# Row softmax on one core: loads 6 and 7 issued by ScalarE, between two loops of exponentials

## The chip, the core and the metric

The kernel runs on one core of a Trainium2 chip. Its engines run beside each other and meet through semaphores: VectorE (DVE in the profile), ScalarE (ACT), GpSimd (POOL), SyncE (SP), and TensorE (PE), which has no part in this kernel. Data moves between the device's memory (HBM) and the core's on-chip memory (SBUF, 128 partitions) by 16 DMA engines. A transfer is issued by an instruction of an engine and goes into a queue of that engine; here SP issues all of them.

The metric is the time on the device in microseconds (us), from runs on the chip. One further execution is profiled; its trace gives the single instructions, the DMA shares, and the span from its first to its last instruction.

## The reference

```python
def reference(x):                      # x: (16, 1024, 512) float32
    x_max = np.max(x, axis=-1, keepdims=True)
    exp_x = np.exp(x - x_max)
    return (exp_x / np.sum(exp_x, axis=-1, keepdims=True)).astype(np.float32)
```

A softmax over the last axis: 16,384 rows of 512 numbers. 33.55 MB are read and as many written.

## The kernel before

**Tiling.** The 16,384 rows are 128 "rows" of each of the 128 partitions. They are cut into 16 groups of 8 (`GROUP`, `GROUPS`), and for the transfers into 8 blocks of 16, so two groups to a block (`BLOCKS`). One transfer moves a block: 128 partitions, 32 KB in one piece for each, 4 MB. The on-chip buffer `held` has room for 12 groups (`RING`, 96 rows), that is 6 blocks. Block 6 goes into the place of block 0, block 7 into that of block 1, when these have been stored. In the text load 6 is the load of rows 96 to 112, load 7 that of rows 112 to 128; store 0 is the store of rows 0 to 16, and so on.

**A group's way.** VectorE takes the negated maximum of each row (`rowmax`, line 171; step M in `VECTOR`) and counts up `maxed`. ScalarE waits for that and does eight exponentials in place with the row's sum beside them (lines 210 to 223; one loop over 16 groups, with the row's place in `held` worked out from the loop's index), and counts up `expd`. VectorE takes the reciprocal of the sums (line 179), and the product of the rows with it (line 185) is made by GpSimd for groups 0 to 11 (steps P) and by VectorE for groups 12 to 15 (steps V). The product counts up `scaled[g]`. The order of VectorE's steps is written out by hand in `VECTOR`; its end is M12 M13 V12 M14 V13 M15 V14 V15.

**SP's queue.** SP issues the transfers in the order of `ORDER`: loads 0 to 5 ahead (`AHEAD`), then stores 0, 1, 2, loads 6 and 7, stores 3 to 7. Before a store it waits until both groups of the block are scaled. `AFTER` adds later groups to wait for: group 4 before store 0, group 8 before load 6, group 9 before load 7, group 11 before store 3, group 12 before store 5. Before load 6 and load 7 it also waits until store 0 and store 1 have landed (lines 152 to 155). At the end it waits for the stores that nothing waited for yet (lines 226 to 228). `take` (line 115) is a wait for a semaphore that takes the count off again; most waits carry that line in the trace.

**Whom the loads serve.** The first maximum of a block waits for its load (`take` in `rowmax`): M12 for load 6, M14 for load 7.

Of the kernel before, what the change touches and what calls it, by code (L numbers as in the profile page):

```python
# [8 lines left out]
EXP = mybir.ActivationFunctionType.Exp  # L9
# [4 lines left out]
GROUP = 8  # L14
GROUPS = 16
RING = 12 * GROUP

# [2 lines left out]
ORDER = [  # L22
    ("L", (0, 16)),
    ("L", (16, 32)),
    ("L", (32, 48)),
    ("L", (48, 64)),
    ("L", (64, 80)),
    ("L", (80, 96)),
    ("S", (0, 16)),
    ("S", (16, 32)),  # L30
# [9 lines left out]
AHEAD = 6  # L40

AFTER = {("S", 0): 4, ("L", 96): 8, ("L", 112): 9, ("S", 48): 11, ("S", 80): 12}

# [28 lines left out]
@with_exitstack  # L77
def kernel(
    ctx: ExitStack,
    tc: tile.TileContext,  # L80
    x: bass.AP,
    out: bass.AP,
):
    nc = tc.nc
    nc.at_finalize(loads_at_the_head)
    P = nc.NUM_PARTITIONS

    d = x.shape[-1]
    x_rows, out_rows = x.flatten_outer_dims(), out.flatten_outer_dims()
    assert x_rows.shape[0] == GROUPS * GROUP * P  # L90

    def in_dram(rows, a, b):

        first, last = next(k for k in BLOCKS if k[0] <= a and b <= k[1])
        block = rows[first * P : last * P].rearrange("(p r) d -> p r d", p=P)
        return block[:, a - first : b - first, :]

    held = nc.alloc_sbuf_tensor("held", [P, RING, d], F32).ap()
    shift = nc.alloc_sbuf_tensor("shift", [P, GROUPS * GROUP], F32).ap()
    sums = nc.alloc_sbuf_tensor("sums", [P, GROUPS * GROUP], F32).ap()  # L100
    recip = nc.alloc_sbuf_tensor("recip", [P, GROUPS * GROUP], F32).ap()

    loads = [k for what, k in ORDER if what == "L"]
    stores = [k for what, k in ORDER if what == "S"]
    loaded = {k: nc.alloc_semaphore(f"loaded{k[0]}") for k in loads}
    scaled = [nc.alloc_semaphore(f"scaled{g}") for g in range(GROUPS)]
    stored = {k: nc.alloc_semaphore(f"stored{k[0]}") for k in stores}
    maxed = nc.alloc_semaphore("maxed")
    expd = nc.alloc_semaphore("expd")
    to_pool = nc.alloc_semaphore("to_pool")  # L110
    to_vector = nc.alloc_semaphore("to_vector")

    def take(engine, semaphore, n):

        engine.wait_ge(semaphore, n).then_inc(semaphore, -n)  # L115

    def rows(a, b):
        assert a // RING == (b - 1) // RING
        return held[:, a % RING : (b - 1) % RING + 1, :]

    def meets(k, a, b):
        return k[0] < b and a < k[1]

    def group(g):
        return g * GROUP, (g + 1) * GROUP

    def stats(t, g):
        return t[:, g * GROUP : (g + 1) * GROUP]

    def load(k):  # L130
        copy = nc.sync.dma_start(out=rows(*k), in_=in_dram(x_rows, *k))
        copy.then_inc(loaded[k], 16)
        return copy

    with tc.manual_schedule():
        for _, k in ORDER[:AHEAD]:
            tc.no_tile_sem_insts.add(load(k).ins.name)  # L140
    tc.close()
    tc.compile()  # L142

    taken, done = set(), set()
    for what, k in ORDER[AHEAD:]:
        for g in range(GROUPS):
            due = AFTER.get((what, k[0])) == g or (what == "S" and meets(k, *group(g)))
            if due and g not in done:
                take(nc.sync, scaled[g], 1)
                done.add(g)  # L150
        if what == "L":
            for s in stores:
                if meets(s, k[0] - RING, k[1] - RING) and s not in taken:
                    take(nc.sync, stored[s], 16)
                    taken.add(s)
            load(k)
        else:
            nc.sync.dma_start(out=in_dram(out_rows, *k), in_=rows(*k)).then_inc(
                stored[k], 16
            )  # L160

    seen, given = set(), {}

    def rowmax(g):
        for k in loads:
            if meets(k, *group(g)) and k not in seen:
                take(nc.vector, loaded[k], 16)
                seen.add(k)  # L170
        nc.vector.reduce_max(  # L171
            out=stats(shift, g), in_=rows(*group(g)), axis=AX, negate=True
        ).then_inc(maxed, 1)

    def scale(g, engine, ready):

        if g == 0:
            take(nc.vector, expd, 1)
        ratio = nc.vector.reciprocal(out=stats(recip, g), in_=stats(sums, g))  # L179
        if g:  # L180
            ratio.wait_op(expd, g, "sem-ge")
        ratio.then_inc(ready, 1)
        if g == 0:
            take(engine, ready, 1)
        product = engine.tensor_mul(  # L185
            out=rows(*group(g)),
            in0=rows(*group(g)),
            in1=stats(recip, g).unsqueeze(2).to_broadcast([P, GROUP, d]),
        )
        if g:  # L190
            given[ready] = given.get(ready, 0) + 1
            product.wait_op(ready, given[ready], "sem-ge")
        product.then_inc(scaled[g], 1)

    for step in VECTOR.split():
        what, g = step[0], int(step[1:])
        if what == "M":
            rowmax(g)
        elif what == "V":
            scale(g, nc.vector, to_vector)  # L200
        else:
            scale(g, nc.gpsimd, to_pool)
    take(nc.vector, expd, GROUPS - 1)
    take(nc.vector, to_vector, given[to_vector])
    take(nc.gpsimd, to_pool, given[to_pool])


    nc.scalar.preload_act_table(EXP)  # L208

    with nc.scalar.Fori(0, GROUPS) as i:  # L210
        take(nc.scalar, maxed, 1)
        for r in range(GROUP):
            row = held[:, bass.ds(i % (RING // GROUP) * GROUP + r, 1), :]
            at = bass.ds(i * GROUP + r, 1)
            act = nc.scalar.activation(  # L215
                out=row,
                in_=row,
                func=EXP,
                bias=shift[:, at],
                scale=1.0,  # L220
                accum_out=sums[:, at],
            )
        act.then_inc(expd, 1)


    for k in stores:
        if k not in taken:
            take(nc.sync, stored[k], 16)
# [30 lines left out]
```

## Time and profile before

| | us |
|---|---|
| median of 3 runs | 159.43 (159.36 to 159.45) |
| the profiled execution | 159.46 |
| its span | 158.1 |
| GpSimd's 12 products | 83.7 |
| VectorE's 16 maxima | 70.3 |
| VectorE's 4 products | 17.7 |
| ScalarE's 128 exponentials | 90.3 |

67.11 MB pass the DMA engines, at a mean of 424 GB/s over the span. In the page, a line's start and length are in us from the first instruction; "L171" is line 171 of the kernel; a name with a q behind the engine is an instruction of its sequencer (issue of a DMA, wait, register). The row marked DMA cuts the span into 40 equal slices and gives, in tenths, how busy the 16 DMA engines were. "us to landing" runs from a transfer's issue until its last byte has arrived, so it contains the time for which the transfer stood behind others in the queue.

### The profile page before, as it was taken

How to read it: one execution, taken by the hardware profiler on the slowest of the kernel's cores; microseconds unless marked ns; L12 is line 12 of the kernel's file. 1: busy time of each engine (PE TensorE's matmuls, PEld its weight loads, DVE VectorE, ACT ScalarE, POOL GpSimd, SP SyncE). 2: the span in 40 equal slices, each digit the busy share in tenths (PEclk: the TensorE clock that was granted, in tenths of full speed). 3: DMA queues.
4: the chain of work that ended last, by engine and by line, in shares of the span. 5: the costliest groups of instructions: out<-in, count | busy, mean ns of one | idle time of the engine just before them, and what ended most of it. 6: DMA issues, size and time to landing. Idle time of an engine off the chain costs nothing. (4 is left out here: it accounts for less than half of the span.)

```text
span 158.1 us, 720 instructions
## 1 busy us (share of the span) xinstructions
DVE 90.0 (57%) x36; ACT 92.0 (58%) x257; POOL 83.9 (53%) x16
## 2 busy tenths in 40 slices
DVE  0008959778977977977700000695999996920000
ACT  0300699999999999999994000049946839000000
POOL 0000009999999999999999999991000000000000
DMA  7999999999999999999999999999999999999996
GB/s 265 439 472 414 406 464 456 398 414 481 431 398 423 472 431 398 423 489 414 398 439 489 381 414 398 439 472 414 398 448 472 406 398 439 481 406 414 464 448 265
DMA packets 2304, 67.11 MB, mean 424 GB/s; under 512 B 256, under 2 KB 256, under 8 KB 256
## 3 DMA queue, kind: packets, MB, share of 16 engines
q1 hardware_dynamic: 2304, 67.11, 99.0%
HBM read 33.55 MB, written 33.55 MB: 424 GB/s over the span
## 5 line engine op out<-in xcount | busy, mean ns | idle before, releaser
L215 ACT ACTIVATE held<-held,shift x128 | 90.3, 709 | 38.7 <-ACTq L115 38.7
L185 POOL TENSOR_TENSOR held<-held,recip 128x4096 f32<-128x4096 f32 x12 | 83.7, 7016 | 23.1 <-POOLq L115 23.1
L171 DVE TENSOR_REDUCE shift<-held 128x8 f32<-128x4096 f32 x16 | 70.3, 4401 | 27.3 <-DVEq L115 27.3
L215 ACT ACTIVATION_READ_ACCUMULATOR held<-held,shift x128 | 24.2, 189 | 0.0
L185 DVE TENSOR_TENSOR held<-held,recip 128x4096 f32<-128x4096 f32 x4 | 17.7, 4425 | 0.1
L179 DVE RECIPROCAL recip<-sums 128x8 f32<-128x8 f32 x16 | 3.2, 202 | 21.9 <-ACT held L215 20.0
L208 ACT ACT_TABLE_LOAD x1 | 1.3, 1283 | 3.9 <-PEq L142 3.9
L243 POOL MEMSET const-float32-0.0<- 128x1 f32 x1 | 0.1, 98 | 0.2 <-issue 0.2
L243 POOL MEMSET const-bfloat16-1.0<- 128x1 bf16 x1 | 0.1, 101 | 0.0
L243 POOL MEMSET const-uint8-127<- 128x1 uint8 x1 | 0.1, 101 | 0.0
L243 POOL MEMSET const-float32-1.0<- 128x1 f32 x1 | 0.1, 98 | 0.0
## 6 DMA issues: line engine op xcount, KB each, us to landing
held<-in_x_dram SPq DMA_DIRECT2D x8, 4096.0 KB, 25.8
out_dram<-held SPq DMA_DIRECT2D x8, 4096.0 KB, 21.2
```

Source lines behind the costliest of these rows:

```text
L171: nc.vector.reduce_max(out=stats(shift, g), in_=rows(*group(g)), axis=AX, negate=True).then_inc(maxed, 1)
L179: ratio = nc.vector.reciprocal(out=stats(recip, g), in_=stats(sums, g))
L185: product = engine.tensor_mul(out=rows(*group(g)), in0=rows(*group(g)), in1=stats(recip, g).unsqueeze(2).to_broadcast([P, GROUP, d]),)
L208: nc.scalar.preload_act_table(EXP)
L215: act = nc.scalar.activation(out=row, in_=row, func=EXP, bias=shift[:, at], scale=1.0, accum_out=sums[:, at],)
L243: nc = _bacc.Bacc("TRN2", target_bir_lowering=False, num_devices=1)
```

## The change

Loads 6 and 7 leave SP's queue. ScalarE issues them in its own queue, after the exponentials of group 11 and before those of group 12; before each of them it waits until the store whose place it takes has landed. The loop of ScalarE over 16 groups becomes two loops, of twelve groups and of four, with a plain index into `held`. SP issues the stores alone, from store 0 on in the same order; its waits for groups 8 and 9 now stand before store 4, as that store's own.

```diff
-AFTER = {("S", 0): 4, ("L", 96): 8, ("L", 112): 9, ("S", 48): 11, ("S", 80): 12}
+AFTER = {(0, 16): 4, (48, 64): 11, (80, 96): 12}
...
-    def load(k):
-        copy = nc.sync.dma_start(out=rows(*k), in_=in_dram(x_rows, *k))
+    def load(k, engine):
+        copy = engine.dma_start(out=rows(*k), in_=in_dram(x_rows, *k))
         copy.then_inc(loaded[k], 16)
         return copy
...
-            tc.no_tile_sem_insts.add(load(k).ins.name)
+            tc.no_tile_sem_insts.add(load(k, nc.sync).ins.name)
...
-    taken, done = set(), set()
+    done = set()
     for what, k in ORDER[AHEAD:]:
+        if what == "L":
+            continue
         for g in range(GROUPS):
-            due = AFTER.get((what, k[0])) == g or (what == "S" and meets(k, *group(g)))
-            if due and g not in done:
+            if (meets(k, *group(g)) or AFTER.get(k) == g) and g not in done:
                 take(nc.sync, scaled[g], 1)
                 done.add(g)
-        if what == "L":
-            for s in stores:
-                if meets(s, k[0] - RING, k[1] - RING) and s not in taken:
-                    take(nc.sync, stored[s], 16)
-                    taken.add(s)
-            load(k)
-        else:
-            nc.sync.dma_start(out=in_dram(out_rows, *k), in_=rows(*k)).then_inc(
-                stored[k], 16
-            )
+        nc.sync.dma_start(out=in_dram(out_rows, *k), in_=rows(*k)).then_inc(
+            stored[k], 16
+        )
...
-    with nc.scalar.Fori(0, GROUPS) as i:
-        take(nc.scalar, maxed, 1)
-        for r in range(GROUP):
-            row = held[:, bass.ds(i % (RING // GROUP) * GROUP + r, 1), :]
-            at = bass.ds(i * GROUP + r, 1)
...
+    def exps(groups, first):
+        with nc.scalar.Fori(0, groups) as i:
+            take(nc.scalar, maxed, 1)
+            for r in range(GROUP):
+                row = held[:, bass.ds(i * GROUP + r, 1), :]
+                at = bass.ds(i * GROUP + first + r, 1)
...
+    exps(RING // GROUP, 0)
+    taken = set()
+    for what, k in ORDER[AHEAD:]:
+        if what == "L":
+            for s in stores:
+                if meets(s, k[0] - RING, k[1] - RING) and s not in taken:
+                    take(nc.scalar, stored[s], 16)
+                    taken.add(s)
+            load(k, nc.scalar)
+    exps(GROUPS - RING // GROUP, RING)
```

The body of the loop, the activation with its sum, is otherwise the same.

More of the change, by code (lines that the diff above doesn't have):

```diff
@@ L208 @@
     nc.scalar.preload_act_table(EXP)
-    with nc.scalar.Fori(0, GROUPS) as i:
-        take(nc.scalar, maxed, 1)
-        for r in range(GROUP):
-            row = held[:, bass.ds(i % (RING // GROUP) * GROUP + r, 1), :]
-            at = bass.ds(i * GROUP + r, 1)
[L215 to L223, printed above, removed]
+    def exps(groups, first):
[4 more added lines that the diff above has]
+                at = bass.ds(i * GROUP + first + r, 1)
+                act = nc.scalar.activation(
+                    out=row,
+                    in_=row,
+                    func=EXP,
+                    bias=shift[:, at],
+                    scale=1.0,
+                    accum_out=sums[:, at],
+                )
+            act.then_inc(expd, 1)
+    exps(RING // GROUP, 0)
[8 more added lines that the diff above has]
+    exps(GROUPS - RING // GROUP, RING)
     for k in stores:
```

## The prediction

> **What bounds the kernel now.** I read the page's head first, then its row of DMA shares, then the queue's part.
>
> ```profile
> span 158.1 us, 720 instructions
> DVE 90.0 (57%) x36; ACT 92.0 (58%) x257; POOL 83.9 (53%) x16
> ...
> DMA  7999999999999999999999999999999999999996
> ...
> q1 hardware_dynamic: 2304, 67.11, 99.0%
> ```
>
> No engine is busy for 60% of the span, while the 16 DMA engines are full in every slice but the first and the last, and one queue accounts for all of it. The kernel is bound by its bytes. The profile's chain that ended last covers only a few us before 139.5 and then stops at the issue of the last store, because it doesn't follow a transfer that waits behind other transfers; so I rebuilt the order of the transfers from the timeline of SP's queue and from each issue's time to landing.
>
> ```profile
> 0.00 3.14 SPq L131 DMA_DIRECT2D held<-in_x_dram  x6
> 58.51 7.30 SPq L158 DMA_DIRECT2D out_dram<-held  x3
> 86.47 7.31 SPq L131 DMA_DIRECT2D held<-in_x_dram  x2
> 107.32 32.48 SPq L158 DMA_DIRECT2D out_dram<-held  x5
> ```
>
> Issue plus time to landing gives: load 0 at 12.2 us, load 5 at 60.8 (2.7 + 58.1), store 0 at 70.5 (58.5 + 12.0), store 1 at 80.1 (59.0 + 21.1), store 2 at 90.4 (65.5 + 24.9), load 6 at 100.0 (86.5 + 13.5), load 7 at 109.7 (93.4 + 16.3), store 3 at 119.4 (107.3 + 12.1), and store 7 at 158.1 (139.5 + 18.6), which is the end of the span. So 16 transfers of 4 MB follow each other at about 9.7 us: 12.2 + 15 x 9.73 = 158.1. Each is issued before its predecessor ends; the closest is store 3, issued at 107.3 while load 7 lands at 109.7, a margin of 2.4 us. A change can move the end only if it leaves the DMA engines without work, or changes what a packet costs them.
>
> Packets do not always cost the same. The windows view (us, engines' busy time, clock, share of the 16 engines, GB/s) around the turns from loads to stores and back:
>
> ```profile
> 0.00:1.00 1.00, 0.00 (x0) 0.00 (x0) 0.20 (x4) 1.00 0.00 0
> 0.00:5.00 5.00, 0.00 (x0) 1.06 (x1) 0.20 (x4) 1.00 0.84 315
> 9.70:19.40 9.70, 7.04 (x2) 2.26 (x7) 0.00 (x0) 1.00 1.00 432
> 58.00:63.00 5.00, 3.90 (x3) 5.00 (x16) 5.00 (x2) 1.00 0.98 419
> 87.00:92.00 5.00, 0.00 (x0) 0.00 (x0) 5.00 (x1) 1.00 0.92 354
> 107.00:112.00 5.00, 3.16 (x3) 5.00 (x17) 0.22 (x1) 1.00 0.97 419
> ```
>
> A row's share x length x 16 is engine time, its GB/s x length is bytes, and a big packet is 32,768 bytes (4096 KB over the 128 of a transfer; 2304 packets are 16 x 144, 128 of them data and 16 of a few bytes). In a steady stretch (9.7 to 19.4): 128 packets in 155.2 us of engine time, 1.21 us each. At 87 to 92, where store 2 gives way to load 6: 1.77 MB are 54 packets in 0.92 x 5 x 16 = 73.6 us, 1.36 us each. The excess, 54 x 0.15 = 8 us over 16 engines, is 0.5 us. At the start, with no store about: 48 packets in 67.2 us, excess 9 us, 0.55 us for each engine. Where a load gives way to a store (58 to 63, 107 to 112): 64 packets in 78.4 and 77.6 us, excess 1 and 0 us, at most 0.06 us. So a beginning stream of loads costs about 0.5 us, with or without stores before it, and a beginning stream of stores costs nothing that shows.
>
> **The change, part by part.** *The two issues move to ScalarE.* SP loses two DMA issues (0.34 us each) and the waits for stored 0 and 1, and takes scaled 8 and 9 later, before store 4. ScalarE gets the two issues and two waits: 2 x 0.34 to 0.49 us (the range of load issues on SP) + 2 x 0.02 (a wait of ScalarE's queue took 17 ns) = 0.7 to 1.0 us. What stands behind them in ScalarE's queue is the exponentials of group 12, for which it waits anyway:
>
> ```profile
> 84.77 0.18 ACT L215 ACTIVATION_READ_ACCUMULATOR held<-held,shift  x1
> ...
> 100.14 8.74 DVE L171 TENSOR_REDUCE shift<-held 128x8 f32<-128x4096 f32 x2 [14.94 <-DVEq L115]
> 104.90 0.72 ACT L215 ACTIVATE held<-held,shift  x1 [19.94 <-ACTq L115]
> ...
> 115.27 4.41 DVE L171 TENSOR_REDUCE shift<-held 128x8 f32<-128x4096 f32 x1
> ```
>
> The waits are open when it comes to them: store 0 landed at 70.5, store 1 at 80.1, the twelfth group ends at 85.0. So both loads are issued by about 86, under 19.94 us of idle time. Cost 0; without that cover, 1 us on the path to group 12.
>
> *The second loop and the plain index.* A few register instructions (29 ns a MOVE, 35 an ALU_OP, 40 to 45 a branch) come and go, under 0.2 us, in the same idle time. If the longer program has to be fetched at the loop's end, no row here prices it; 0 below, and above the 4.5 us from 85 to 90.4 would pass unseen, since store 2 still has work. I take 0. The second queue may cost something at the start or end of the program. What lies outside the span is 159.46 - 158.1 = 1.4 us in all; nearest are SP's waits at the barrier, 0.4 us, so 0 to 0.4; I take 0, as nothing in the loop's issue touches the barrier.
>
> *When SP's stores go.* Store 0 still waits for scaled 4, stores 1 and 2 for scaled 3 and 5, store 3 for scaled 11 (POOL, 12 x 7.0 us from 23.5, to 107.2). SP no longer waits between, but store 3 had its wait last at 107.3 already. Gain 0.
>
> *Two queues at once.* This is the only part that reaches the bound. The first bytes moved not before 1.0 us after the first issue (the window 0 to 1), so load 6 comes into play at 86.1, and store 2 has 90.4 - 86.1 = 4.3 us of work left. If both queues share evenly, store 2 lands near 94.7 instead of 90.4; nobody waits for it but the end. Load 6 has then done 4.3 of its 9.7 us, goes on alone, and lands at 100.0 as before. Load 7 goes alone until store 3 comes in at 107.3 + 1.0 = 108.3 with 1.4 us of it left: it lands at 111.1 instead of 109.7. Who waits for load 7 is the maximum of group 14, at 115.27, held there by VectorE's own product of group 12; 4.2 us of cover remain. Had it none, 1.4 us would pass down the chain to store 7, whose issue at 139.5 lies 8.9 us ahead of 148.4, where store 6 ends. Cost 0. The Trainium skill, in "DMA: Bandwidth & Descriptors" (Queues, rings and completion order), says that each engine goes round the queues that have work, one packet each; by that rule the sharing is even and the landings are these, and no run shown has two data queues at once. The Trainium skill, on that page (Issuing engines are not separate DMA queues), says that a second issuing engine saves only issue time; by that the sum is 0, as here.
>
> What a packet costs while both queues are at work is not in the trace. Below: the loads begin under a running store stream and the whole 0.5 us at 87 to 92 goes, -0.5. Above: each return from a store's packet to a load's costs as much as the one return at 87 to 92. Shared packets per engine are 4.3 / 1.21 + 1.4 / 1.21 = 4.7 returns; 4.7 x 0.5 = 2.35, less the 0.5 already paid, +1.85. I take 0: the start shows the 0.5 us without any store, so it belongs to a stream that begins, and one stream of loads still begins, once. The turns from load to store, where engines of both kinds run beside each other for some tenths of a us, show no excess.
>
> **Sum.** 0 (issues) + 0 (loop) + 0 (stores) + 0 (sharing) on the profiled 159.46 (span 158.1); the runs' median is 159.43, so it is typical. Forecast 159.4.
>
> **Rivals.** *The beginning of the loads is hidden.* For it: load 6 starts 4.3 us earlier, beside a store that keeps each engine busy. Against: at 87 to 92 the load had been issued before store 2 ended and still paid. 159.4 - 0.5 = 158.9.
>
> *Returning to loads costs (the other side).* Engines alternate packet by packet from 86.1 to 94.7 and from 108.3 to 111.1. For it: the only return in the trace cost 0.5 us. Against: the start's 0.55 without stores. The kernel is slower as soon as a return costs over 0.5 / 4.7 = 0.11 us; at 0.17 it is +0.3 (159.75), at 0.5 +1.85 (161.3). I put its middle at 160.3.
>
> *The stores' queue goes first.* Then load 7's last 1.4 us wait behind stores 3, 4 and 5 (3 x 9.7 from 108.3) until about 138.8. Groups 14's maximum (4.4), VectorE's product 13 (4.4 + 0.2), maximum 15 (4.4), the exponentials of 15 (5.7), product 15 (4.6) put store 7's issue at 162.5; 1.0 + 9.7 more is a span of 173, a time of 174.5. Nothing in the rows speaks for it. If the loads go first, load 6 and 7 come 5 us sooner, store 2 later, and the time stays.
>
> *The change doesn't do what it says* if ScalarE's issues came after 90.4; the waits above exclude it, and the time would be the same until 5 us later still.
>
> **Chances.** The forecast 0.42, beginning hidden 0.22, returns cost 0.33, stores first 0.03. Over 0.2% (0.32 us) is about what a measurement can tell from no change. So faster 0.22, same 0.42, slower 0.33 + 0.03 = 0.36. The range goes from 158.8 (the hidden case, 0.1 for scatter) to 160.9 (most of the returns' case); outside are the upper third of that case, the stores-first case and a little below, some 0.16. The forecast's own range is 159.1 to 159.7.
>
> **What would show it.** Two load issues on ScalarE's queue at 85 to 86; store 2's time to landing up from 24.9 to about 29, load 7 landing near 111, group 14's maximum still at 115.3; the DMA row without a dip. In the hidden case the window 87 to 92 goes from 0.92 and 354 GB/s to some 430. In the returns' case GB/s falls in 86 to 95 and again in 108 to 111, and everything behind it shifts by the same amount. It would be wrong if the shared stretch lost over 0.3 us, or if the time outside the span grew.

## The result, and the profile after

The changed kernel takes 160.24 us (median of 6 runs, 159.95 to 160.59), the kernel before, run beside it, 159.44: a ratio of 1.0048, 95% interval 1.0031 to 1.0065. It is slower by 0.8 us, where no change was forecast. The profiled execution took 159.96 us, with a span of 158.6 where before had 158.1. It is one of the two fastest of the six, so its trace shows 0.5 of the 0.8 us.

The page of the changed kernel, its head and its DMA queues:

```profile
span 158.6 us, 721 instructions
DVE 90.0 (57%) x36; ACT 92.0 (58%) x257; POOL 83.9 (53%) x16
...
DMA  7999999999999999999999999999999999999996
...
q1 hardware_dynamic: 2016, 58.72, 86.7%
q10 hardware_dynamic: 288, 8.39, 12.4%
q14 instruction: 1, 0.01, 0.0%
```

The engines' work is the same to 0.1 us and the DMA row still has no dip. What is new is the queue q10, ScalarE's, with the two loads, and one fetch of instructions (q14). The timeline of the issues, with the last instruction of group 11's exponentials:

```profile
81.01 0.38 ACTq L131 DMA_DIRECT2D held<-in_x_dram  x1
...
81.51 1.18 ACTq L131 DMA_DIRECT2D held<-in_x_dram  x1
...
84.81 0.19 ACT L212 ACTIVATION_READ_ACCUMULATOR held<-held,shift  x1
...
107.35 3.25 SPq L152 DMA_DIRECT2D out_dram<-held  x2
```

ScalarE's sequencer issued the loads at 81.0 and 81.5, while its exponentials ran until 85.0: it runs ahead of them, and store 1 had landed at 80.2. Issue plus time to landing: store 2 at 95.4 (65.5 + 29.9; before 90.4), load 6 at 100.4 (before 100.0), load 7 at 110.1 (109.7), store 3 at 119.9 (119.4), store 7 at 158.6 (158.1). So 0.4 us were there by load 6's end and 0.5 by store 3's. The windows view shows where:

```profile
58.00:63.00 5.00, 3.90 (x3) 5.00 (x16) 5.00 (x2) 1.00 0.97 419
82.00:87.00 5.00, 0.20 (x1) 3.00 (x10) 5.00 (x2) 1.00 0.93 328
87.00:92.00 5.00, 0.00 (x0) 0.00 (x0) 5.00 (x1) 1.00 1.02 439
92.00:97.00 5.00, 0.00 (x0) 0.00 (x0) 5.00 (x2) 1.00 1.02 439
...
107.00:112.00 5.00, 3.20 (x3) 5.00 (x15) 0.25 (x1) 1.00 0.99 408
```

Read as in the prediction (share x length x 16 over the packets that the GB/s make): 82 to 87 has 50 packets in 74.4 us, 1.49 us each instead of 1.21, which is 0.86 us lost for each engine; 107 to 112 has 62 packets in 79.2 us, 1.28 each, 0.25 us lost. Load 6's first packet starts at 85.6, and store 2's last at 92.7; of that stretch the view of the queues says:

```profile
q10 hardware_dynamic: 46, 1.51, 52.5%
q1 hardware_dynamic: 44, 1.44, 47.0%
```

So load 6 had 46 packets and store 2 had 44, and followed engine by engine they alternate one by one. From 87 to 97 a packet costs 1.22: alternating is free. The slow packets start at 84 to 86: they are store 2's last ones ahead of the alternating and load 6's first. Before, the one loss was 0.5 at 87 to 92. So load 6's beginning lost 0.86 instead of 0.5, and store 3's beginning 0.25 instead of 0.

### The profile page after: what moved, and what is told of

Its sections match the earlier page's. It is cut to its first block, busy times and chain, and to the rows that moved or that the text cites. A ratio compares the mean times of both kernels' runs of the same rounds, so it can differ in the third digit from the quotient of the medians.

```text
span 158.6 us, 721 instructions
## 1 busy us (share of the span) xinstructions
DVE 90.0 (57%) x36; ACT 92.0 (58%) x257; POOL 83.9 (53%) x16
## 3 DMA queue, kind: packets, MB, share of 16 engines
q1 hardware_dynamic: 2016, 58.72, 86.7%
```

## The experiments

Lost time below is the sum over a stretch's big packets of what each took above 1.213 us (a packet of a steady stretch), divided by 16 engines, from the packets in each trace. It comes from one execution of each kernel, the ratio from 4 to 12 runs. Six kernels have load 6 in SP's queue at 86.4 to 86.7 and stores 0 to 2 ahead of it at the old times (before, e1, e4, e6, e8, e11); they lost 0.33 to 0.55 at load 6, so two traces that differ by 0.2 there show no difference. "Before" in each comparison is the kernel before, run beside the other.

| kernel | ratio to before (95%) | lost at load 6's beginning | lost at store 3's | elsewhere |
|---|---|---|---|---|
| before | 1 | 0.48 | 0 | |
| the change | 1.0048 (1.0031 to 1.0065) | 0.87 | 0.23 | |
| e1 | 0.9999 (0.9989 to 1.0009) | 0.35 | 0 | |
| e2 | 1.0044 (1.0027 to 1.0060) | 0.42 | 0.53 | |
| e3 | 1.0072 (1.0049 to 1.0096) | 0.85 | 0.39 | |
| e4 | 0.9999 (0.9990 to 1.0008) | 0.53 | 0 | |
| e5 | 0.9996 (0.9987 to 1.0005) | 0.35 | 0 | |
| e6 | 1.0121 (1.0106 to 1.0137) | 0.33 | engines idle | |
| e7 | 1.0217 (1.0200 to 1.0235) | 0.46 | 0.60 | store 7 issued late |
| e8 | 1.0060 (1.0040 to 1.0080) | 0.33 | 0 | 0.26 at the small loads |
| e9 | 1.0046 (1.0033 to 1.0059) | 0 | 0.23 | 0.62 before store 0 |
| e10 | 1.0003 (0.9994 to 1.0011) | 0.44 | 0 | |
| e11 | 1.0001 (0.9992 to 1.0010) | 0.55 | 0 | |
| e12 | 1.0066 (1.0047 to 1.0085) | 0.52 | 0.48 | |
| e13 | 1.0030 (1.0016 to 1.0045) | 0.69 | 0 | |
| e14 | 1.0054 (1.0041 to 1.0068) | 0.02 | 0 | 0.81 before store 0 |
| e15 | 1.0039 (1.0025 to 1.0052) | 0.76 | 0 | |
| e16 | 1.0077 (1.0064 to 1.0091) | 0.9 | 0.02 | 0.2 at the small loads |
| e17 | 1.0007 (0.9998 to 1.0016) | 0.27 | 0 | |

### First round: the queue, the loops, the moments

**e1, two loops alone.** The kernel before with the change's `exps` and its two calls, and nothing between them.

> The kernel before with ScalarE's loop cut into two, nothing else; SP issues loads 6 and 7 as before. Theory (a queue that begins beside another one at work costs: some 0.3 us at load 6, some 0.3 us at store 3): as before, 159.4. Rival (the longer program: the profile after the change has one fetch of instructions at 108.9 us, next to store 3's slow packets): the fetch is there and the time is near that of the change, 160.0 to 160.3.

159.50 against 159.49. The fetch of instructions is in its trace (at 108.8 us) and costs nothing that the time shows. The loops and the longer program are out.

**e2, ScalarE's queue at the old times.**

```diff
...
+            take(nc.scalar, scaled[8 if k[0] == RING else 9], 1)
             load(k, nc.scalar)
...
```

In the lines left out SP no longer waits for groups 8 and 9.

> The change, but ScalarE waits for group 8's product before load 6 and for group 9's before load 7, so both go out when SP sent them in the kernel before (86.5 and 93.5), in ScalarE's queue. Load 6 then reaches the engines at about 88, when store 2 has at most one packet left on each. Theory (the queue that begins anew): the cost of store 3's start stays, that of load 6 stays too, 160.0 to 160.4. Rival (the moment: load 6 starts while store 2 has several packets to go on every engine): load 6's part goes, store 3's stays, about 159.7. If both go (159.4), only the moment counts.

160.19. The loads go out at 86.3 and 93.3, as before, and only the queue is another; nearly the whole 0.8 us is there. The windows view of this kernel:

```profile
83.00:88.00 5.00, 0.20 (x1) 1.91 (x6) 5.00 (x2) 1.00 1.02 439
88.00:97.00 9.00, 0.00 (x0) 0.00 (x0) 9.00 (x2) 1.00 1.03 422
...
107.00:112.00 5.00, 3.19 (x3) 5.00 (x15) 0.15 (x1) 1.00 0.99 382
```

58 packets in 79.2 us at 107 to 112 are 1.37 us each, 0.55 us lost; load 6's loss is back at before's size. So load 6's extra is not there when it begins at the old time, and store 3's loss is there without it. The time was as the theory had it, its division was not: here store 3 alone makes the 0.7 us.

**e3, store 3 earlier.** `AFTER` with `(48, 64): 10` instead of 11.

> The change, but store 3 waits for group 10 instead of 11, so it is issued at 100.3 instead of 107.3, when load 7 has 9 us to go. Store 3 and load 7 then alternate from 101.5; load 7 lands near 118, group 14's maximum starts some 2.5 us later, inside the 8.9 us that store 7 has to spare. Theory: if store 3's 0.3 us is a wait for a queue to come up after its engines have run out of loads, the engines have loads meanwhile and it goes: 0.3 below the change. Rival (two streams that meet lose a burst whatever is left): the slow packets move to 101 to 104 and the time is that of the change.

160.81, where the change had 160.24; the intervals of the two ratios overlap, so it is no faster than the change, and more isn't shown. Every engine was on a packet of load 7 when it came:

```profile
88.00:102.90 14.90, 2.23 (x1) 0.00 (x0) 14.90 (x3) 1.00 0.98 422
102.90:104.00 1.10, 1.10 (x1) 0.00 (x0) 1.10 (x1) 1.00 1.45 477
```

The 16 packets that began between 102.9 and 104.0 took 1.45 x 1.1 x 16 / 16 = 1.6 us each instead of 1.21, 2.4 us after store 3's issue at 100.6, and the packets before and after them took 1.21. So it isn't that engines ran out of loads: they were stopped while they had work. The theory of a mere start-up wait fell.

**e4, one queue, both loads together.** `AFTER` of the kernel before without `("L", 112): 9`.

> The kernel before, with load 7 issued straight behind load 6 at 86.5, both in SP's queue. Theory (a second queue costs): as before, 159.4. Rival (two loads waiting at the engines at once make the beginning of the loads dearer): 0.3 above before, 159.7, with more lost time in the stretch 84 to 92.

159.47 against 159.49. Two loads at once cost nothing in SP's queue.

### Second round: which beginnings cost

**e5, the hand-over once.** On e2: SP stops after store 2, and ScalarE issues the rest in its own queue.

```diff
...
+    for g, ks in (12, stores[3:5]), (13, stores[5:6]), (14, stores[6:7]), (15, stores[7:]):
+        exps(1, g * GROUP)
+        for k in ks:
+            store(k, nc.scalar)
...
```

> Loads 6 and 7 in ScalarE's queue at the times of the kernel before (after groups 8 and 9), and stores 3 to 7 behind them in the same queue, between single groups of exponentials; SP's queue ends with store 2. No queue begins again beside one at work, except ScalarE's with load 6, in store 2's last packets. Theory (what costs is a queue that has run empty and begins again beside another: store 3 on SP's): store 3's 0.3 to 0.5 us goes and the time is 159.4 to 159.6. Rival (a second data queue costs in itself, or stores behind loads of ScalarE's queue do): 160.2, as with the two loads alone at these times.

159.43, the time of before. Its window at store 3's beginning:

```profile
107.00:112.00 5.00, 3.37 (x3) 5.00 (x15) 0.36 (x1) 1.00 0.98 421
```

64 packets in 78.4 us, 1.22 each: nothing lost. The same loads in the same queue at the same times as in e2, and the 0.7 us are gone when store 3 follows load 7 in one queue. This is the plainest of the runs: a second queue in itself costs nothing here; going back to the first one does.

**e6, only the stores on ScalarE's queue.** The kernel before, with stores 3 to 7 issued as in e5 and the loads left in SP's queue.

> The kernel before with loads 6 and 7 left in SP's queue and stores 3 to 7 issued by ScalarE, at the same times. Only one queue begins beside another: ScalarE's with store 3, under load 7's last packets. Theory: store 3's start costs 0.3 to 0.5 us as it does on SP's queue after the change, 159.8 to 160.0, with the lost time in 107 to 112 and the 0.5 at 87 to 92 as before. Rival (only SP's queue, once emptied, or only loads on ScalarE's queue cost): 159.4.

161.40, far beyond either number. ScalarE's queue had never been used, and the issue of store 3 at 107.24 took 2.94 us. The windows of this kernel:

```profile
107.00:109.00 2.00, 1.80 (x1) 2.00 (x7) 0.13 (x1) 1.00 0.62 266
109.00:110.50 1.50, 0.11 (x1) 1.36 (x4) 0.00 (x0) 1.00 0.00 0
110.50:112.00 1.50, 1.47 (x2) 1.14 (x3) 0.00 (x0) 1.00 1.40 590
```

No packet begins from 109.0 to 110.5: load 7 had run out, store 3 wasn't there yet. Its first packets come 3.4 us after the issue began and 0.5 us after it ended, where in one queue a store issued at 107.3 followed load 7 at about 109 with no gap. The margin of 2.4 us that is enough in a queue at work was not enough for ScalarE's unused one. In the change, SP's idle queue had its first packet of store 3 at 108.8, 1.5 us after the issue, and no engine stood idle.

**e7, SP's queue never empty.** `AFTER` with `(64, 80): 11` instead of `(48, 64): 11`, so store 3 is queued at 79.4, behind store 2.

> The change with store 3 queued behind store 2 at 79.5 (it waits for groups 6 and 7 alone) and store 4 at group 11's product (107.3), so SP's queue never runs empty; loads 6 and 7 alternate with stores 2, 3 and 4 from about 84 to 124. Load 7 lands near 124, group 14 starts there, and store 7 is issued near 149 instead of 140, about 1 to 1.5 us too late, so the time goes to 161 to 162. What counts is the packets: theory, no lost time between 92 and 140, as no queue begins there, and alternating stays free; rival (alternating costs over a longer stretch, or store 3's start costs whatever the queue holds), 0.3 us or more lost per engine there.

162.88; store 7 was issued at 150.3, so the time itself says nothing here. The packets do:

```profile
88.00:94.00 6.00, 0.00 (x0) 0.00 (x0) 6.00 (x2) 1.00 1.01 437
94.00:96.00 2.00, 0.00 (x0) 0.00 (x0) 2.00 (x1) 1.00 0.91 262
96.00:112.00 16.00, 5.42 (x2) 0.69 (x2) 11.19 (x2) 1.00 1.04 451
```

Between 94 and 96, where store 2 ends and store 3 begins in SP's queue, 16 packets took 1.82 us each, 0.6 us lost per engine, although that queue had not been empty. So "a queue that has run empty" is not the condition either. Alternating stays free (1.21 us a packet before and after it), and store 4's beginning at 114 lost nothing.

**e8, five small starts.** The kernel before with five loads of 8 KB on ScalarE's queue between its groups.

> The kernel before, with five small loads (16 partitions x 512 bytes, 8 KB, into a buffer nobody reads) issued by ScalarE between groups 2, 4, 6, 8 and 10, while SP's queue is at work. By their bytes they are worth 5 x 0.02 us. Theory in its strong form (any start of an empty queue beside a busy one stalls every engine some 0.4 us): 5 x 0.4 = 2 us, 161.4. Weak form (the stall belongs to the start of a large transfer): 159.4 to 159.7.

160.30, between the forms. The packets lost 0.26 us in all, chiefly on the large packets around the third small load (51 to 53 us). Their first packets came 3.5, 3.4, 3.6, 1.5 and 4.5 us after their issues. Small starts cost, but not 0.4 us each. How 0.26 us of packets make 0.9 us of time, from four runs, is open.

### Third round: counting transfers, and a warm queue

By then the losses lay at a queue's first transfer or at the tenth of SP's, in nearly every trace. Four runs tried that.

**e9, load 0 in halves.** `ORDER` begins with `("L", (0, 8)), ("L", (8, 16))`, and `AHEAD` is 7.

> The kernel before with load 0 as two transfers of half the size, so store 2, not load 6, is the tenth transfer of SP's queue. New theory (the tenth transfer of a queue makes its engines lose some 0.3 to 0.6 us, whatever it is; so does a queue's first): the lost time of 87 to 92 moves to store 2's beginning, 78 to 84, none is left at load 6, and the time stays at 159.4. Rival (it belongs to a stream of loads that begins after stores): it stays at 87 to 92.

160.35, and the loss is at none of the two places: 0.62 us lie at 57 to 60, on load 5's packets before store 0, and load 6's beginning lost nothing. GpSimd's products come earlier in this kernel, so store 0 was queued at 54.7 instead of 58.5, and store 3 at 103.5 instead of 107.3; at store 3 the loss is 0.23, with no second queue in the kernel.

**e10, the hand-over once with a warm queue.** On e5, one load of 8 KB first in ScalarE's queue.

> Loads 6, 7 and stores 3 to 7 in ScalarE's queue at the times of before (the hand-over once), with one small load (8 KB into a buffer nobody reads) first in ScalarE's queue, ahead of the exponentials. SP's queue has nine transfers, ScalarE's eight. New theory: no tenth transfer, and the first of ScalarE's queue is the small one, which keeps no engine long; load 6's 0.35 goes: 159.1, faster than before by 0.3. Rival (load 6 pays for the turn from stores to loads): 159.4 to 159.5, with the loss at 87 to 92 in place.

159.58 against 159.57; load 6 lost 0.44. A queue's first use was not its cause.

**e11 and e12, a small load in SP's queue** behind load 5, in the kernel before and in the change.

```diff
...
+    nc.sync.dma_start(
+        out=scratch[0:16, :], in_=in_dram(x_rows, 0, 1)[0:16, 0, 0:128]
+    ).then_inc(small, 16)
...
```

> The kernel before with one small load (8 KB) in SP's queue behind load 5. It counts as one transfer but as 2 packets for each engine instead of 9. If transfers are counted, store 2 is the tenth and the loss moves to 78 to 84. If packets are counted (the 82nd of a queue is the first of the tenth big transfer), it comes with store 2's eighth data packet, at 87 to 89, and hardly moves. Time 159.4 to 159.5 either way.

> The change with the same small load in SP's queue behind load 5, so store 2, not store 3, is SP's tenth transfer. New theory, if transfers are counted: store 3's loss at 107 to 112 goes and one at 78 to 84 comes, the time stays at 160.0 to 160.4. Old theory (SP's queue has run empty and begins again): the loss at 107 to 112 stays where it is.

159.59 against 159.57, with the loss still at load 6; and 160.50, with store 3's loss still at 108 (0.48). Store 2, now the tenth, lost nothing in either. Counting transfers fell, by e9, e11 and e12.

### Fourth round: moments, and the two terms apart

**e13 and e17, load 6 queued earlier in one queue.** The kernel before without its waits for groups 8 and 9 (e13), and with group 7 for load 6 (e17).

> The kernel before without its waits for groups 8 and 9 ahead of loads 6 and 7: load 6 goes into SP's queue at 70.5 (store 0 landed), load 7 at 80.2, with 20 us and 10 us of store 2's block still ahead of load 6. Theory A (engines lose some 0.4 us about 2.5 us after an issue that reaches a queue nearly run out): the loss at 87 to 92 goes, 159.0. Theory B (it belongs to the turn from stores to loads): the loss stays, 159.4. Theory C (the tenth transfer of SP's queue, by its packets): stays, 159.4.

> The kernel before with load 6 queued after group 7 (79.5) instead of group 8 (86.5), load 7 after group 9 as before. Load 6 then waits in SP's queue for 10 us before its turn. With load 0 in halves it waited 7.4 us and no time was lost at 87 to 92; queued 19 us ahead it lost more than before (159.8). Theory (the moment decides): between the two, 159.0 to 159.8 and other than before by over 0.2. Rival (the moment of load 6 alone doesn't matter; load 0 in halves had paid its loss at store 0 already): 159.4 to 159.5.

Queued at 70.9, load 6 loses more (0.69) and the kernel takes 159.81 against 159.44; queued at 79.4 it lost 0.27, hardly outside the 0.33 to 0.55 of the old moment, and the time was 159.59 against 159.48, no difference. Neither is faster than before.

**e14, store 0 queued earlier.** `AFTER` of the kernel before without `("S", 0): 4`.

> The kernel before without the wait for group 4 ahead of store 0: store 0 goes into SP's queue at 37.5, store 1 at 51.5, with loads still to come ahead of them. With load 0 in halves, store 0's issue at 54.7 came with 0.6 us lost at 57 to 61. Theory (the moment of an issue against the work under way decides): a loss of some 0.5 us appears before 60, 159.9. Rival (that loss came from the halves): 159.4.

160.24, in one queue. Store 0 was queued at 37.5, store 1 at 51.4, and the loss comes where loads give way to stores:

```profile
56.00:62.00 6.00, 4.54 (x2) 6.00 (x17) 6.00 (x2) 1.00 1.02 382
```

70 packets in 97.9 us, 1.40 each, 0.8 us lost, and load 6 lost nothing (0.02) although it was queued at 86.4 as before. So the wait for group 4 in the kernel before is worth 0.8 us, without any second queue: a turn between loads and stores costs or not by when the next transfer is queued. The traces with one queue agree at the turns from loads to stores: a store queued 2.2 to 2.7 us before the load ahead of it landed lost nothing (before, e1, e4, e11, e13, e17, store 3 of e14), one queued 6.7 to 24 us before it lost 0.2 to 0.8 (e9 at stores 0 and 3, e14 at store 0). That is what the traces have in common, not a rule that was tested.

**e15, the hand-over at the change's time.** On e5, without the waits for groups 8 and 9 ahead of the loads.

> The hand-over once, with loads 6 and 7 issued at the change's own time (81.0 and 81.5, when ScalarE's sequencer reaches them), and stores 3 to 7 behind them in ScalarE's queue. So store 3 begins nothing new, and only load 6's part of the change is left. Theory (two terms: load 6 beginning beside four packets of store 2, +0.4 over before, and store 3 on SP's idle queue, +0.25 to 0.5): +0.4, 159.8 to 159.9. Rival (only store 3's term is real): 159.4. Rival (only load 6's): 160.2.

160.21 against 159.44: load 6's term alone is nearly as dear as the whole change (the ratio gives 0.6 us, the medians 0.8). e5 is the same kernel with the loads issued at 86.6 and 93.5, and takes the time of before, so the moment of the loads alone makes the difference. The windows view of e15, and below it one line of e5's:

```profile
83.00:88.00 5.00, 0.20 (x1) 2.05 (x6) 5.00 (x2) 1.00 1.05 387
...
107.00:112.00 5.00, 3.38 (x3) 5.00 (x15) 0.31 (x1) 1.00 0.98 421
...
83.00:88.00 5.00, 0.20 (x1) 2.10 (x6) 5.00 (x2) 1.00 1.07 459
```

59 packets in 84 us at 83 to 88, 0.77 us lost per engine; nothing at 107 to 112. In e5 the same stretch has 70 packets in 85.6 us, 1.22 each. I had split the 0.8 us between two terms that would add up. In the change they don't: by the ratios e2 has store 3's alone and costs 0.7, e15 load 6's alone and costs 0.6, and the change has both and costs 0.8, short of 1.3. But e3 and e12, which also have both, cost 1.1, each to within 0.4, so how far the two add is not fixed.

**e16, SP's queue kept awake.** On the change, 8 KB on SP's queue after groups 8, 9 and 10.

> The change with three small loads (8 KB) in SP's queue after groups 8, 9 and 10 (86.5, 93.5, 100.5), so its idle time before store 3 is 4 us instead of 12. Theory (a queue idle for long has to be started again): store 3's loss at 107 to 112 falls to 0, 159.9. Rival (any start beside another queue): it stays, and the small ones add up to 0.2 us, 160.2 to 160.5.

160.68. Store 3's loss did go (0.02), as the theory had it, yet the time did not fall: the small loads lost 0.2 and load 6 0.9. It settles nothing on the time.

## Why the prediction was wrong

**What held.** The kernel is bound by its bytes, and the engines' work had no part in it. Load 6 landed at 100.4 (predicted 100.0), store 2 at 95.4 (about 94.7), and group 14's maximum began at 115.67, held by VectorE as before. The loop and the longer program cost nothing (e1). The queues did share evenly: from 85.6 to 92.7 the engines took 46 packets of load 6 and 44 of store 2, in turn. The Trainium skill, in "DMA: Bandwidth & Descriptors" (Queues, rings and completion order), says that each engine goes round the queues that have work, packet by packet; the trace agrees, with these counts. Load 7 landed at 110.1 and not at 111.1, because it never shared: each engine took its first packet of store 3, from 108.8 on, only when it had run out of load 7.

**The issues at 85 to 86** were wrong by 4 us: they came at 81.0, because the sequencer issues while earlier exponentials still run. I took "after the twelfth group" for the end of its work. A second error hid it: I gave the first packet 1.0 us after the issue, and it took 4.6. So load 6 came into play at 85.6, near the 86.1 of the prediction, and the landings came out right by luck. The moment of the issue mattered all the same: e5, with the loads at 86.6 and 93.5, takes the time of before, and e15, with them at 81.1 and 81.6, 0.6 to 0.8 us more. The packets say it less plainly: with load 6 issued at 81 in ScalarE's queue the loss there was 0.46 to 0.90 over six kernels (the change, e3, e7, e12, e15, e16).

**The step that failed** is "Two queues at once", at "I take 0". The reason given there, that the 0.5 us belongs to a stream of loads that begins and "one stream of loads still begins, once", took the turn as a fixed price. It is none: a stream of loads begins at load 6 in all these kernels, and lost 0 to 0.9 there (0 in e9, 0.02 in e14, 0.87 in the change), and at the turns from loads to stores, which I had priced at nothing, 0 to 0.8, in one queue too (e14). The change altered both turns: load 6 begins while store 2 has 44 of its 128 packets still to start, and store 3 comes from a queue that had nothing to do for 12 us. In place of the 0, the trace has 0.87 us lost at load 6, where before had 0.48, and 0.23 at store 3, and the time is 0.8 us longer. The Trainium skill, in "DMA: Bandwidth & Descriptors" (Issuing engines are not separate DMA queues), says that a second issuing engine saves only issue time. The trace agrees in that nothing was gained; the time, 160.24 us against 159.44, is a loss on top of that.

**The rival "returning to loads costs"** had the right sign and nearly the size (160.3 at its middle), for a reason that is refuted: alternating costs nothing (e7 too, over 16 us). That it came near is luck, and the range held the measured time only by way of this rival.

**Why two losses need not add up.** The end is that of the slowest engine, and each has its own 128 packets. Following the packets engine by engine in the traces (each is put behind the one that ended where it starts): before, all end between 157.1 and 157.8. In e15 eleven end by 157.7, as before, and five at 158.1 to 158.6; four of those lost 1.2 us on a single packet of store 2 at 85.5, and the last of them 0.3 more behind the fetch of instructions at 110. In the change the last one lost 0.54 at 84.2 and 0.87 at 109.0. Where another engine is hit by the second loss, it hides behind the first.

**What is shown and what is open.** Shown: the change's cost is not that of the loops (e1), of two loads queued together (e4) or of load 6 queued 7 us earlier in one queue (e17). It comes from each of the two beginnings in the second queue alone (e2, e15), and with load 6 at its old time and all that follows in the same queue it is gone (e5). A loss of this kind is not bound to a second queue, though: in one queue e13 costs 0.4 to 0.5 us, and e9 and e14 0.7 to 0.9. Not settled: why engines stop once at such a beginning. An emptied queue (e7), the lack of other work (e3), a queue's first use (e10) and the number of the transfer (e9, e11, e12) are ruled out as the one condition; the moment at which the next transfer is queued matters (e13, e14, and e5 beside e15), but in one queue load 6 lost 0.69 us when queued at 70.9, 0 at 82.7 (e9), and 0.02 (e14) to 0.55 (e11) at 86.4 to 86.7, and I have no rule for it. No version was faster than the kernel before.

## What to carry to other kernels

Where transfers already follow each other without a gap, another queue has nothing to give, and each turn between queues or between loads and stores could here cost each DMA engine, on the mean, up to 0.9 us once; price it by packets around the turns, not by the mean GB/s. If a second queue is used, hand over once instead of going back and forth (e5), and not while the first still has several packets to go (e15). Until the first packet of a queue that wasn't at work, these traces had 1.4 to 4.8 us, and not the 1.0 of the program's start. Waits ahead of a DMA that look idle (group 4 before store 0) can be worth more than they delay, so take one away only with a measurement.

## What the runs showed of the hardware that I had not expected

- Two queues at work on the same 16 engines, one with loads and one with stores, alternate one packet each at no cost: 1.22 us a packet, against 1.21 alone.
- A packet for another queue can begin late: 3.4 to 3.6 us after the issue for the first three small loads of e8, 4.6 for load 6 of the change, 3.4 in e6, where it left all engines idle for 1.5 us. It was 1.5 us for store 3 in SP's queue, idle for 12 us before.
- The second of two issues close together can hold its sequencer: 1.18 us for load 7 and 2.73 us for store 4 after the change, against 0.34 and 0.43 for the same two before. It is not bound to the second queue: load 7 straight behind load 6 in SP's queue took 1.10 us (e4).
- ScalarE's sequencer issued a DMA 4 us before the exponentials ahead of it in the program were done.
